# A pad of 192 bytes instead of 64 in front of the second phase's buffers: the spacing of matmuls whose weights load beside them

## The chip, the cores and the metric

The kernel runs on one core of a Trainium2 chip. What counts is the device time of one execution in microseconds, here the median of several runs. A second, profiled execution left the trace from which the rows below are taken. TensorE is called PE for its matmuls and PEld for its weight loads, VectorE DVE, ScalarE ACT, GpSimd POOL and SyncE SP.

## The reference, cut to what matters

One decoder layer on 512 positions of width 2048, all in float32. It mixes along time with a gated recurrence and with eight pairs of recurrent heads, then comes a feed-forward network of width 6144, then a gated embedding:

```python
h = h + jnp.concatenate([out_a, out_b], axis=-1) @ w_o[i]
u = rmsnorm(h, ln_ffn[i])
gate = causal_dwconv(u @ w_gate[i], conv_f_w[i], conv_f_b[i])
h = h + (jax.nn.gelu(gate) * (u @ w_up[i])) @ w_down[i]
u = rmsnorm(h, ln_ple[i])
e = jax.nn.sigmoid(u @ w_ple_gate[i]) * (p[i] @ w_ple_proj[i])
h = h + rmsnorm(e, ln_ple_post[i])
...
return rmsnorm(h, ln_final)
```

The change touches buffers of the last part alone: from the end of `w_o` to the final norm.

## The kernel before, in words

**Products.** Every large float32 product is made of three products of a shorter type: each operand is split into a high part, which ACT rounds (L138 for weights, L151 or L154 for activations), and a low part, which DVE makes as the difference (L139, L152, L155). PE then does high times high, high times low, low times high. Each of these three matmuls has its own weight load of 128 by 128 values, 512 bytes in each partition. PE loads the weights of the next matmul while the present one streams its moving operand.

**Stages.** Phase 1 is the mixing with its input products. Phase 2 starts with the second half of `w_o`, and has these stages:

- The gate and up products (`part`, L1281 to L1283). They are done by a scheme with seven products of quarters instead of eight. For each of 48 blocks of 128 columns there are seven units (`q5`, `p1`, `p4`, `p6`, `p7`, `p2`, `p3`), each with 8 steps of three matmuls. The stationary operand is a tile of weights (`whi`, `wlo`, or the pair x12 and x15). The moving operand is a form of the activations, 256 columns (1,024 bytes), and lies in the tiles s0 to s27. That is 48 x 7 x 24 = 8,064 matmuls.
- The down product (`product`, L1407 to L1409), 680 x 3 matmuls of 512 columns. Here the activations, in tiles s0 to s20, are stationary, and the weights `whi` and `wlo` move.
- The embedding's gate (`gate`, L1548 to L1550): activations stationary, most of them in s tiles and two of the sixteen in x13 and x14, weights moving. Three of the four column blocks are 512 wide, the last is done in two halves of 256.

**Where the tiles lie.** The memory of a partition is laid out by pools, one behind the other: `wp` with `whi` and `wlo`, `bp` with x0 to x15, then the pool of the phase, `k1` or `k2`; another pool stands at the far end. The tiles named here are 4,096 bytes each and follow without gaps. In the built program the first `whi` begins at byte 640, x0 at 25,216, and `k2` at 90,752, so that all three are at 128 modulo 256. The first thing in `k2` is a tile that nothing reads or writes, `skew` (L1227). It is 64 bytes long, and so all tiles behind it, s0 to s27 and the two buffers `e` among them, begin at 192 modulo 256. The offsets inside these tiles are multiples of 512 bytes, so that every operand of the three stages begins at the same place modulo 256 as its tile.

The order of the instructions is written out by hand in some stages and made by a scheduler with priorities in the others; the weights come by DMA from the SP and POOL queues, three units ahead.

Of the kernel before, what the change touches and what calls it, by code (L numbers as in the profile page):

```python
# [4 lines left out]
F32 = mybir.dt.float32  # L5
# [84 lines left out]
class Builder:  # L90
# [1125 lines left out]
    def phase2(self):  # L1216
        nc, A, k2 = self.nc, self.A, self.k2
# [6 lines left out]
        acc = self.t(self.cp, "row", (128, S + 2), bufs=1)[:, 0:S]  # L1224
        self.LOOK = 3
        hd = [self.dp.tile([128, 2, S], F32, name="hd%d" % i) for i in range(8)]
        self.skew = k2.tile([128, 16], F32, name="skew")  # L1227
        KIND = ("q5", "p1", "p4", "p6", "p7", "p2", "p3")
        X = {u: [T("s%d" % (4 * i + j), 1, (128, 2, 2, 256), F32R) for j in range(4)] for i, u in enumerate(KIND)}
        halves = lambda t: (t[:, 0:256], t[:, 256:512])  # L1230
# [513 lines left out]
```

## Time and profile before

| | us |
|---|---|
| three runs | 2582.25, 2549.99, 2585.5 |
| their median | 2582.25 |
| the profiled execution's own time | 2587.38 |
| its span, from the first to the last instruction | 2585.6 |
| PE busy | 2531.7 |
| DVE busy | 1902.7 |
| ACT busy | 1250.2 |

By stages, from the trace: phase 1 and the rest of `w_o` end at about 907 us, the gate and up products run from 907 to 1868 us, the down product from 1868 to 2372 us, the embedding and the final norm from 2372 us to the end.

A matmul's row in the trace shows a start and a duration. The durations overlap: a matmul of 256 columns is shown with 0.28 us, while the next starts 0.12 us later. So the rate of PE is read from the distance of the starts, or from a count of rows in a stretch in which PE is never idle, not from the duration of one row.

### The profile page before, as it was taken

What the parts mean: (1) busy time and instruction counts of PE and PEld (TensorE: products, weight loads), DVE (VectorE), ACT (ScalarE), POOL (GpSimd) and SP (SyncE); (2) the same over time, 40 slices, a digit from 0 to 9 for tenths busy, and PEclk for the clock granted to TensorE, in tenths of its full rate; (3) what the DMA queues carried; (4) which work ended last, traced back from release to release, by engine and by line L of the source; (5) the groups of instructions that cost most, each with busy time, mean ns of one, the idle gap of its engine ahead of it and who ended that gap; (6) DMA issues with size and microseconds to landing.
All of it is one profiled execution on the core that took longest, in us unless ns stands there. A gap on an engine that the chain in (4) does not pass through costs nothing.

```text
span 2585.6 us, 51614 instructions
## 1 busy us (share of the span) xinstructions
PE 2531.7 (98%) x21922; PEld 2221.2 (86%) x21922; DVE 1902.7 (74%) x2603; ACT 1250.2 (48%) x1735; POOL 228.3 (9%) x251
## 2 busy tenths in 40 slices
PE   9989999999999989999999999999999999999997
PEld 8867777777777889999999999999977878788887
DVE  5765775676675988888888887888876787896447
ACT  6563654547432644444444444444465453534345
POOL 0010100101031000000000000000000000000001
PEclk9989999999999999999999999999999999999999
DMA  7321222222342577767777667777678686843223
GB/s 255 94 70 59 87 78 67 79 87 71 98 137 87 172 209 185 190 168 197 188 187 193 187 170 195 193 187 196 188 214 252 180 228 179 237 117 115 93 91 111
DMA packets 131303, 393.76 MB, mean 152 GB/s; under 512 B 14464, under 2 KB 26624, under 8 KB 131072
## 3 DMA queue, kind: packets, MB, share of 16 engines
q1 hardware_dynamic: 96480, 299.22, 34.3%
q0 software_dynamic: 19872, 72.36, 16.8%
q10 hardware_dynamic: 14720, 18.88, 2.2%
q8 instruction: 171, 2.80, 0.4%
q14 instruction: 60, 0.49, 0.1%
HBM read 353.97 MB, written 36.44 MB: 151 GB/s over the span
## 4 chain that ended last, share of the span: by engine, by line
PE 68%; issue 18%; DVE 5%; ACT 5%; POOL 2%; DMA 1%; SPq 0%; POOLq 0%; ACTq 0%; DVEq 0%
PE mm L1282 8%; PE mm L1281 8%; PE mm L1283 8%; PE mm L168 5%; PE mm L170 5%; PE mm L172 5%; PE wk L1282 3%; PE wk L1281 3%; PE wk L1283 3%; PE mm L1548 2%; PE mm L1549 2%; PE mm L1550 2%; PE wk L833 1%; PE mm L1408 1%; PE mm L1409 1%
## 5 line engine op out<-in xcount | busy, mean ns | idle before, releaser
L138 ACT ACTIVATE whi<-x 128x1024 fp32r<-128x1024 f32 x329 | 349.0, 1061 | 481.6 <-PE mm L1282 222.8
L139 DVE TENSOR_TENSOR wlo<-x,whi 128x1024 fp32r<-128x1024 f32 x329 | 402.4, 1224 | 140.4 <-ACT whi L138 136.8
L138 ACT ACTIVATE whi<-wraw 128x1024 fp32r<-128x1024 f32 (+1 forms) x229 | 233.2, 1018 | 389.7 <-PE mm L170 186.4
L139 DVE TENSOR_TENSOR wlo<-wraw,whi 128x1024 fp32r<-128x1024 f32 (+1 forms) x229 | 278.3, 1215 | 174.6 <-ACT whi L138 173.2
L1281 PE MATMUL mm<-s,whi 128*128 128x256 f32 x1432 | 399.8, 279 | 2.4 <-ACT s L151 1.2
L1282 PE MATMUL mm<-s,whi 128*128 128x256 f32 x1432 | 401.0, 280 | 0.2 <-DVE s L152 0.2
L1283 PE MATMUL mm<-s,wlo 128*128 128x256 f32 x1432 | 399.7, 279 | 0.8 <-DVE wlo L139 0.8
L168 PE MATMUL mm<-x,whi 128*128 128x512 f32 x832 | 333.0, 400 | 1.4 <-DVE hT L458 0.9
L172 PE MATMUL mm<-x,wlo 128*128 128x512 f32 x832 | 332.7, 400 | 0.0
L170 PE MATMUL mm<-x,whi 128*128 128x512 f32 x832 | 331.0, 398 | 0.0
L1408 PE MATMUL mm<-wlo,s 128*128 128x512 f32 x680 | 270.5, 398 | 2.8 <-DVE wlo L139 2.8
L1281 PEld LDWEIGHTS mm<-s,whi 128*128 128x128 f32 x1432 | 269.2, 188 | 2.9 <-ACT s L151 1.4
L1407 PE MATMUL mm<-whi,s 128*128 128x512 f32 x680 | 269.6, 398 | 1.7 <-ACT whi L138 1.2
L1409 PE MATMUL mm<-whi,s 128*128 128x512 f32 x680 | 270.2, 397 | 0.1
L1282 PEld LDWEIGHTS mm<-s,whi 128*128 128x128 f32 x1432 | 268.8, 188 | 0.4 <-DVE s L152 0.4
L1283 PEld LDWEIGHTS mm<-s,wlo 128*128 128x128 f32 x1432 | 267.8, 187 | 1.0 <-DVE wlo L139 1.0
L168 PEld LDWEIGHTS mm<-x,whi 128*128 128x128 f32 x832 | 157.5, 189 | 37.3 <-issue 3.0
L170 PEld LDWEIGHTS mm<-x,whi 128*128 128x128 f32 x832 | 157.6, 189 | 33.9 <-issue 1.8
L172 PEld LDWEIGHTS mm<-x,wlo 128*128 128x128 f32 x832 | 157.2, 189 | 33.9 <-issue 1.9
L1281 PE MATMUL wk<-s,whi 128*128 128x256 f32 x584 | 163.9, 281 | 2.9 <-DVE e L1307 2.9
L1148 POOL DMA_DIRECT2D x<-wgu x94 | 82.7, 880 | 936.3 <-DVE wlo L139 638.6
L1282 PE MATMUL wk<-s,whi 128*128 128x256 f32 x584 | 164.2, 281 | 0.0
(588 smaller groups left out, 5415.1 us busy)
## 6 DMA issues: line engine op xcount, KB each, us to landing
x<-wgu SPq DMA_DIRECT2D x144, 512.0 KB, 4.2
x<-wgu POOLq DMA_DIRECT2D x94, 512.0 KB, 5.5
wraw<-wz SPq DMA_DIRECT2D x80, 512.0 KB, 3.5
wraw<-wgu SPq DMA_DIRECT2D x51, 512.0 KB, 4.4
x<-wd SPq DMA_DIRECT2D x49, 512.0 KB, 5.8
x<-wd POOLq DMA_DIRECT2D x44, 512.0 KB, 5.6
wraw<-wpg SPq DMA_DIRECT2D x31, 512.0 KB, 3.6
wraw<-wd SPq DMA_DIRECT2D x30, 512.0 KB, 4.5
```

Of the source, the lines that this page charges most:

```text
L138: nc.scalar.activation(hi, raw, AF.Copy)
L139: nc.vector.tensor_tensor(lo, raw, hi.bitcast(F32), ALU.subtract)
L168: nc.tensor.matmul(ps, hi[:, k, :], xh, start=first and i == 0, stop=False)
L170: nc.tensor.matmul(ps, hi[:, k, :], xl, start=False, stop=False)
L172: nc.tensor.matmul(ps, lo[:, k, :], xh, start=False, stop=last and i == n - 1)
L1148: nc.gpsimd.dma_start(g["s"], src(0, 0 if u == "p6" else 1), accum_op=ALU.add)
L1281: TE.matmul(ps, wh[:, k, :], xh, start=k == 0, stop=False)
L1282: TE.matmul(ps, wh[:, k, :], xl, start=False, stop=False)
L1283: TE.matmul(ps, wl[:, k, :], xh, start=False, stop=k == 7)
L1407: TE.matmul(ps, x[0][:, k, ts_], w[0][:, k, :], start=first and k == 0, stop=False)
L1408: TE.matmul(ps, x[0][:, k, ts_], w[1][:, k, :], start=False, stop=False)
L1409: TE.matmul(ps, x[1][:, k, ts_], w[0][:, k, :], start=False, stop=last and k == 1)
```

## The change

The tile `skew` is 48 values long instead of 16, which is 192 bytes instead of 64:

```diff
@@ -1224,7 +1224,7 @@
         acc = self.t(self.cp, "row", (128, S + 2), bufs=1)[:, 0:S]
         self.LOOK = 3
         hd = [self.dp.tile([128, 2, S], F32, name="hd%d" % i) for i in range(8)]
-        self.skew = k2.tile([128, 16], F32, name="skew")
+        self.skew = k2.tile([128, 48], F32, name="skew")
         KIND = ("q5", "p1", "p4", "p6", "p7", "p2", "p3")
         X = {u: [T("s%d" % (4 * i + j), 1, (128, 2, 2, 256), F32R) for j in range(4)] for i, u in enumerate(KIND)}
         halves = lambda t: (t[:, 0:256], t[:, 256:512])
```

Every tile of `k2` moves up by 128 bytes. In the built programs:

| tiles | before, byte | modulo 256 | after, byte | modulo 256 |
|---|---|---|---|---|
| whi, wlo, x0 to x15 | 640, 25,216 and on | 128 | the same | 128 |
| s0 to s27 | 90,816 and on | 192 | 90,944 and on | 64 |
| e (two buffers) | 205,504 and 209,600 | 192 | 205,632 and 209,728 | 64 |
| small tiles of the last stage | 213,696 and on | | 128 bytes higher | |

No instruction is added, removed or moved: the lists of all five engines are the same, row for row. Only the addresses of operands in `k2` differ.

## The prediction

> **What bounds the kernel now.** I read the page first, for the engine that is never idle, then a table of stages, then starts of matmuls.
>
> ```profile
> span 2585.6 us, 51614 instructions
> PE 2531.7 (98%) x21922; PEld 2221.2 (86%) x21922; DVE 1902.7 (74%) x2603; ACT 1250.2 (48%) x1735; POOL 228.3 (9%) x251
> core 0: us, PE busy (x) PEld busy (x) DVE busy (x) ACT busy (x) POOL busy (x), PEclk, DMA share, GB/s
> 907.00:950.00 43.00, 36.11 (x283) 34.87 (x281) 32.38 (x46) 17.79 (x27) 4.75 (x5) 0.96 0.72 215
> 950.00:1868.00 918.00, 918.00 (x7797) 918.00 (x7796) 757.37 (x840) 418.27 (x447) 79.93 (x92) 1.00 0.71 187
> 1868.00:2372.00 504.00, 499.41 (x2186) 400.03 (x2185) 387.97 (x433) 247.47 (x322) 38.76 (x44) 1.00 0.70 194
> 2372.00:2586.00 214.00, 197.19 (x1049) 167.34 (x1046) 112.84 (x199) 88.07 (x166) 7.19 (x8) 0.97 0.30 96
> ```
>
> The second window row is the one that matters: for 918 us, in the gate and up products, PE is never idle and its clock is full (1.00). 7,797 matmuls in 918 us are one every 117.7 ns. Nobody makes PE wait there, and DVE is at 757 of 918 us, or 83%. So this stage lasts exactly as long as PE needs from one start to the next. The down product is alike (499.4 of 504 us).
>
> The change moves no instruction, so its effect can only be in how long one takes. The question is whether the distance of two starts depends on where the operands lie. First, what overlaps with what; from the gate stage:
>
> ```profile
> 1199.83 0.28 PE L1281 MATMUL mm<-s,x 128*128 128x256 f32 x1
> 1199.84 0.19 PEld L1282 LDWEIGHTS mm<-s,x 128*128 128x128 f32 x1
> 1199.95 0.28 PE L1282 MATMUL mm<-s,x 128*128 128x256 f32 x1
> 1199.95 0.19 PEld L1283 LDWEIGHTS mm<-s,x 128*128 128x128 f32 x1
> ```
>
> The load for the next matmul starts with the present one, so each matmul reads two streams: its moving operand and the next one's weights. I call "relation" the place of the weights minus the place of the moving operand, modulo 256 bytes. In the gate stage the weights lie at 128 and the s tiles at 192: relation -64. In the down product and the embedding's gate the roles are exchanged, stationary s tiles at 192 and moving weights at 128: relation +64. The change turns -64 into +64 in the first and +64 into -64 in the other two.
>
> The trace of before has both relations at both widths. The last column block of the embedding's gate has 256 columns: relation +64 for s tiles, and 0 where both operands are s tiles:
>
> ```profile
> 2525.80 0.28 PE L1549 MATMUL mm<-wlo,s 128*128 128x256 f32 x1
> ...
> 2529.45 0.28 PE L1550 MATMUL mm<-whi,s 128*128 128x256 f32 x1
> ...
> 2530.35 0.38 PE L1548 MATMUL mm<-whi,s 128*128 128x256 f32 x1 [0.50 <-ACT e L1555]
> ...
> 2531.49 0.28 PE L1548 MATMUL mm<-whi,s 128*128 128x256 f32 x1
> ...
> 2541.92 0.28 PE L1548 MATMUL mm<-whi,s 128*128 128x256 f32 x1
> ...
> 2547.85 0.28 PE L1550 MATMUL mm<-s,s 128*128 128x256 f32 x1
> ...
> 2548.09 0.28 PE L1549 MATMUL mm<-s,s 128*128 128x256 f32 x1
> ...
> 2548.45 0.28 PE L1549 MATMUL mm<-s,s 128*128 128x256 f32 x1
> ...
> 2550.29 0.28 PE L1550 MATMUL mm<-whi,s 128*128 128x256 f32 x1
> ...
> 2551.99 0.28 PE L1550 MATMUL mm<-whi,s 128*128 128x256 f32 x1
> ```
>
> From 2525.80 to 2529.45 us there are 31 distances in 3.65 us: 117.7 ns. From 2531.49 to 2541.92 there are 92 in 10.43 us: 113.4 ns, with the same relation +64. At relation 0 (the rows `mm<-s,s`) there are 5 distances in 0.60 us: 120 ns. So the same form has three spacings, and +64 alone has been seen at two. Between the slower and the faster run at +64 stands one wait, for ACT, at 2530.35 us. The faster one holds until the relation changes. The last two rows are from the first of the last four passes, behind matmuls at relation 0: 15 distances in 1.70 us, again 113.3 ns.
>
> Now 512 columns. The first two rows are from the down product, relation +64; the other two from the gates of the recurrence in phase 1 (L1021 to L1025), whose moving operands lie at 192 and whose weights at 128, relation -64:
>
> ```profile
> 2107.86 0.39 PE L1409 MATMUL mm<-whi,s 128*128 128x512 f32 x1
> ...
> 2109.26 0.39 PE L1409 MATMUL mm<-whi,s 128*128 128x512 f32 x1
> ...
> 277.70 0.39 PE L1021 MATMUL wk<-lxh,whi 128*128 128x512 f32 x1
> ...
> 281.13 0.39 PE L1021 MATMUL wk<-lxh,whi 128*128 128x512 f32 x1
> ```
>
> 6 distances in 1.40 us are 233.3 ns at +64; 15 distances in 3.43 us are 228.7 ns at -64.
>
> **The change part by part.** The counts come from these groups; every one of their matmuls is there three times, on three lines:
>
> ```profile
> L1281 PE MATMUL mm<-s,whi 128*128 128x256 f32 x1432 | 399.8, 279 | 2.4 <-ACT s L151 1.2 <-ACT whi L138 1.2
> L1281 PE MATMUL wk<-s,whi 128*128 128x256 f32 x584 | 163.9, 281 | 2.9 <-DVE e L1307 2.9
> L1281 PE MATMUL mm<-s,x 128*128 128x256 f32 x488 | 136.2, 279 | 0.0
> L1281 PE MATMUL wk<-s,x 128*128 128x256 f32 x184 | 51.4, 279 | 0.0
> L1407 PE MATMUL mm<-whi,s 128*128 128x512 f32 x680 | 269.6, 398 | 1.7 <-ACT whi L138 1.2 <-ACT s L151 0.6
> L1548 PE MATMUL mm<-whi,s 128*128 128x512 f32 x168 | 66.7, 397 | 0.0
> L1548 PE MATMUL mm<-whi,s 128*128 128x256 f32 x96 | 26.8, 279 | 0.5 <-ACT e L1555 0.5
> L138 ACT ACTIVATE whi<-x 128x1024 fp32r<-128x1024 f32 x209 | 221.9, 1062 | 319.1 <-PE mm L1282 222.8 <-PE wk L1282 95.6 <-ACT x L1327 0.6
> ```
>
> Gate and up: 1432 + 584 + 488 + 184 = 2,688 on each of three lines, 8,064 in all, now 117.7 ns apart. At +64 the trace gives 113.4 or 117.7 ns, so the gain is 8,064 x 4.3 = 35 us or nothing. I take 113.4, because the longer stretch has it and the later pass settles at it, and because this stage runs 918 us without a wait that could throw it out. -35 us is the lower end; the third spacing, 120 ns, would add 8,064 x 2.3 = 19 us and is the upper end.
>
> Is there cover for a PE that is 4% faster? DVE would go from 83% to 86% of the stage and DMA from 0.71 to 0.74. The last row above, of ACT's weight splits between 950 and 1868 us, says that ACT was idle 319 us in front of them and waited for PE to give buffers back: the splits stand ready ahead of PE. So I cost this at nothing; if the cover went, the starts of the gate products would again carry waits as in the 43 us before 950.
>
> Down: 3 x 680 = 2,040 matmuls from 233.3 to 228.7 ns, -9.4 us. The row for -64 comes from stretches of a few us only; the ends are 0 and -9.4, and I take the measured one.
>
> Embedding's gate: 3 x 168 = 504 of 512 columns, -2.3 us by the same prices. 3 x 96 = 288 of 256 columns go to -64, whose spacing is the gate stage's 117.7; most of them have 113.4 now: +1.2 us. Those at relation 0 stay there, since both operands move together or neither does. DVE, ACT and DMA work on the moved tiles is unchanged in form and runs beside PE; I cost it at nothing, since in the gate stage none of it sets PE's time.
>
> Sum: -35 - 9.4 - 2.3 + 1.2 = -45.5 us. The profiled execution's own time is 2587.4 us, so it would be 2542. It lies 5 us above the median of the three runs, 2582.25, and so I forecast 2537 us for the median.
>
> [...]
>
> **The rivals.** The forecast, with the gate stage at 113.4 ns: chance 0.50.
>
> Stuck at 117.7: the two spacings at +64 show that something besides the relation decides, such as the moment at which a run of matmuls begins. The gate stage begins once, near 950 us, and keeps its spacing for 918 us, so it could be stuck in the slower one. Then only down and the embedding gain: 2582 - 10 = 2572 us. For it: the first of the three stretches at +64 above. Against it: the two later ones. Chance 0.24.
>
> No effect: place does not matter, or only modulo 128, where +64 and -64 are the same; the differences above would then come from what the matmuls work on. 2582 us. Against it: the three spacings appear within 25 us in one loop. [...] Chance 0.12.
>
> Slower: the pattern repeats at 512 bytes instead of 256. The gate stage's new relation is then 320, which no row shows at 256 columns, and it might behave as relation 0 does. It decides in the gate stage alone, and from the first matmul on: 8,064 x 2.3 = +19, less the 10 of the other stages (whose new relation, 192 modulo 512, is that of the phase 1 rows): 2591 us. Against it: the phase 1 and down rows fit modulo 256 as well. Chance 0.09.
>
> Both fast: the last 5% is that down goes further, to its width's share of the best spacing, 2 x 113.4 = 226.8 ns: another 2,040 x 1.9 = 4 us, 2533 us.
>
> **How the numbers follow.** The likeliest case is 2537. About 2% of 2582 is 52 us, which is about what a measurement here can tell from no change: faster means under 2530.6, slower over 2633.9. The three runs before lie 35 us apart, as much as the gate stage's whole gain, so runs of either spacing could mix; I allow 10 us to either side of the main case. From 2527 to 2583 the range holds the forecast, the stuck case and the case without effect; the slower rival and the far end of the main case are left out. Faster by over 2%: a third of the best case and a fifth of the main one, 0.12. Slower by over 2% would need the gate stage at over 124 ns, which no row shows: 0.03. The rest, 0.85, is within 2%.
>
> **What would show it.** In the trace of after: a stretch of the gate stage in which PE is never idle, with some 882 matmuls per 100 us (113.4 ns) instead of 850; a gate stage of about 926 us instead of 961; the down product at 228.7 ns; the last block's matmuls with s tiles at 117.7; phase 1 unchanged. The prediction is wrong if the gate stage stays at 117.7 or goes to 120, or if PE shows waits for DVE's `wlo` there.

## The result and the profile after

Twenty runs of each kernel, side by side: a median of 2581.64 us before and 2545.5 us after. The ratio is 0.986, with an interval from 0.983 to 0.989; by a bound of 2% that is no change. Eleven of the runs after lie between 2534 and 2547 us and nine between 2573 and 2582; before, 18 lie between 2577 and 2586 and two at 2546 and 2550. The ratio goes by the eleven alone, and leaves out the five longest of before; the means over all twenty are 2557.4 and 2578.8 us, a ratio of 0.992. That the same program has two times some 35 us apart is what the experiments take up.

The profiled execution took 2540.15 us, 47.2 less than the one of before (2587.38). The head of its page:

```profile
span 2538.4 us, 51614 instructions
PE 2480.6 (98%) x21922; PEld 2180.4 (86%) x21922; DVE 1899.3 (75%) x2603; ACT 1249.2 (49%) x1735; POOL 227.4 (9%) x251
```

PE is as full as before (98%), with as many matmuls, and 51 us less busy. The table of stages of after, with the same columns as before:

```profile
core 0: us, PE busy (x) PEld busy (x) DVE busy (x) ACT busy (x) POOL busy (x), PEclk, DMA share, GB/s
907.00:950.00 43.00, 35.57 (x286) 34.40 (x286) 31.87 (x39) 15.63 (x20) 4.86 (x5) 0.96 0.65 172
950.00:1830.00 880.00, 880.00 (x7754) 879.48 (x7753) 746.73 (x833) 414.11 (x441) 79.81 (x91) 1.00 0.74 195
1830.00:2330.00 500.00, 491.27 (x2187) 398.48 (x2185) 389.96 (x436) 249.41 (x326) 38.76 (x44) 1.00 0.71 196
```

The second row holds the gate and up products and the first 3 us of the down product. PE is never idle there, its clock is full (1.00), and 7,754 matmuls take 880 us. The starts of single matmuls show the spacing, and where it changes (timeline of after, PE; start and duration in us, line, tiles):

```profile
910.21 0.28 PE L1283 MATMUL mm<-s,wlo 128*128 128x256 f32 x1
...
913.04 0.28 PE L1283 MATMUL mm<-s,wlo 128*128 128x256 f32 x1
...
942.13 1.05 PE L210 MATMUL wk<-con,rsr 128*128 128x128 f32 x8
942.94 0.37 PE L1281 MATMUL wk<-s,x 128*128 128x256 f32 x1
943.15 0.28 PE L1282 MATMUL wk<-s,x 128*128 128x256 f32 x1
...
1826.92 0.28 PE L1283 MATMUL mm<-s,x 128*128 128x256 f32 x1
```

From 910.21 to 913.04 us there are 24 distances in 2.83 us: 117.9 ns, the spacing of before. Then come waits and other matmuls. The last of these are the eight of L210. Behind them a stretch begins that runs without a break from 943.15 to 1826.92 us: 7,798 distances in 883.77 us, 113.3 ns. In before, the last stretch of 7,798 begins behind the same L210 and runs at 117.8 ns. From its first matmul to its last, the gate and up stage lasts from 900.2 to 1826.9 us, 926.7 us; before it lasted from 907.1 to 1868.6, 961.4 us.

The down product and the last block of the embedding, from the same timeline:

```profile
2049.83 0.39 PE L1407 MATMUL mm<-whi,s 128*128 128x512 f32 x1
...
2052.35 0.39 PE L1409 MATMUL mm<-whi,s 128*128 128x512 f32 x1
...
2482.91 0.28 PE L1549 MATMUL mm<-wlo,s 128*128 128x256 f32 x1
...
2494.92 0.28 PE L1550 MATMUL mm<-whi,s 128*128 128x256 f32 x1
```

11 distances in 2.52 us are 229.1 ns (233.3 before). 102 distances in 12.01 us are 117.7 ns, at the relation that the gate stage had before.

### The profile page after: what moved, and what is told of

Read it like the earlier page. It is cut to its first block, busy times and chain, and to the rows that moved or that the text cites. A ratio compares the mean times of both kernels' runs of the same rounds, so it can differ in the third digit from the quotient of the medians.

```text
span 2538.4 us, 51614 instructions
## 1 busy us (share of the span) xinstructions
PE 2480.6 (98%) x21922; PEld 2180.4 (86%) x21922; DVE 1899.3 (75%) x2603; ACT 1249.2 (49%) x1735; POOL 227.4 (9%) x251
## 4 chain that ended last, share of the span: by engine, by line
PE 59%; DVE 6%; DMA 3%; ACT 2%; issue 1%; POOL 0%; ACTq 0%; POOLq 0%; DVEq 0%; SPq 0%
PE mm L1283 8%; PE mm L1281 8%; PE mm L1282 8%; PE mm L1409 5%; PE mm L1408 5%; PE mm L1407 5%; PE wk L1281 3%; PE wk L1283 3%; PE wk L1282 3%; PE mm L1548 2%; PE mm L1549 2%; PE mm L1550 2%; DVE wlo L139 2%; DMA wraw<-wd 2%; PE mm L168 1%
## 5 line engine op out<-in xcount | busy, mean ns | idle before, releaser
L138 ACT ACTIVATE whi<-wraw 128x1024 fp32r<-128x1024 f32 (+1 forms) x229 | 233.1, 1018 | 383.8 <-PE mm L170 168.6
L1281 PE MATMUL mm<-s,whi 128*128 128x256 f32 x1432 | 395.6, 276 | 2.7 <-ACT whi L138 2.0
L1282 PE MATMUL mm<-s,whi 128*128 128x256 f32 x1432 | 395.5, 276 | 0.2 <-DVE s L152 0.2
L1407 PE MATMUL mm<-whi,s 128*128 128x512 f32 x680 | 265.4, 392 | 4.1 <-ACT whi L138 2.9
L1409 PE MATMUL mm<-whi,s 128*128 128x512 f32 x680 | 268.6, 395 | 0.2
```

The lines of the kernel that those rows point to most:

```text
L138: nc.scalar.activation(hi, raw, AF.Copy)
L1281: TE.matmul(ps, wh[:, k, :], xh, start=k == 0, stop=False)
L1282: TE.matmul(ps, wh[:, k, :], xl, start=False, stop=False)
L1407: TE.matmul(ps, x[0][:, k, ts_], w[0][:, k, :], start=first and k == 0, stop=False)
L1409: TE.matmul(ps, x[1][:, k, ts_], w[0][:, k, :], start=False, stop=last and k == 1)
```

## The experiments

Distances below are means over a stretch, read from the starts of matmuls as above. All kernels here compute all that the kernel before computes; what is added writes to a column that nothing reads, or to a place that the real products write over afterwards.

### Starting the stretch 144 times

The long stretch starts once, so one execution shows one outcome. A matmul of one column, of the identity and a column of ones, in front of each of the 144 units `p1`, `p6` and `p7` breaks it up:

```diff
-                at = g[u] = (self.mm() if u == "p1" else self.aux())[:, 0:256]
+                bank = self.mm() if u == "p1" else self.aux()
+                at = g[u] = bank[:, 0:256]
+                TE.matmul(bank[:, 256:257], self.K("ident"), self.K("ones1"), start=True, stop=True)
```

Once with the pad of 192 bytes, relation +64:

> Pad of 192 bytes, and in front of every p1, p6 and p7 unit of the gate and up products a one-column float32 matmul into an unused column (its result is not used): 144 restarts of PE's stream in one run. Theory A (the relation allows two spacings and the start of a run of matmuls picks one): of the stretches between two restarts some stand at 113.3 ns and some at 117.7, more of the first. Theory B (the relation alone sets the spacing, and the 35 us between runs come from somewhere else): all stretches at 113.3. Theory C (the spacing wanders in time for a reason outside the kernel): stretches change in the middle, not at restarts. Time: some 144 x 0.1 to 0.3 us more than the kernel after.

and once with the pad of 64, relation -64:

> The same restarts with the pad of 64 bytes. Theory A: most stretches at 117.8 ns, a few at 113.3 (two of twenty runs of the kernel before were some 35 us faster). Theory B: all at 117.8.

Both were run once, with a profile. With the pad of 192 it took 2571.28 us, with the pad of 64 2593.43. Two windows rows, of PE alone; first the pad of 192:

```profile
1000.00:1800.00 800.00, 800.00 (x7040) 1.00 0.71 188
```

and the pad of 64, with the timeline around one of the added matmuls (L1304):

```profile
1000.00:1800.00 800.00, 800.00 (x6926) 1.00 0.70 184
```

and from its timeline:

```profile
1028.04 0.28 PE L1281 MATMUL mm<-s,whi 128*128 128x256 f32 x1
...
1035.82 0.28 PE L1281 MATMUL mm<-s,whi 128*128 128x256 f32 x1
...
1036.17 0.28 PE L1304 MATMUL mm<-con 128*128 128x1 f32 x2
...
1036.73 0.28 PE L1281 MATMUL mm<-s,x 128*128 128x256 f32 x1
...
1039.45 0.28 PE L1281 MATMUL mm<-s,whi 128*128 128x256 f32 x1
```

Ahead of the added matmul are 66 distances in 7.78 us, 117.9 ns; behind it 24 distances in 2.72 us, 113.3 ns. The next added matmul puts it back. With the pad of 64 the stretches alternate in this way nearly throughout, about 75 at 117.8 and 69 at 113.3. The expectation, most slower and a few faster, missed that. With the pad of 192, 142 of 144 run at 113.3, behind faster stretches and once behind a slower one; the other two lie in the first 40 us of the stage, where PE still has waits. By itself the run with the pad of 192 fits a relation that sets the spacing alone nearly as well. But relation -64 has both spacings, and they change where a stretch starts anew. The times are not those of a better kernel: the gate stage lasts 963.1 us with the pad of 192, against 926.7 with its spacing unbroken, so each break costs about 36.4 / 144 = 0.25 us.

### One start, chosen

Twelve extra matmuls stand in front of the last unit at which the stretch begins, (1, `p7`), behind L210. In lead A both operands are the weights' tile, in lead B both are the s tile. So with A, when the real products begin, the moving operand goes to another place; with B the stationary one does. The real products start from zero over the same place.

```diff
-        def part(ps, u):
+        def part(ps, u, lead=0):
             wh, wl = self.wnext()
+            for k in range(lead):
+                TE.matmul(ps, wh[:, k % 8, :], wh[:, 2 * (k % 4):2 * (k % 4) + 2, :].rearrange("p a b -> p (a b)"), start=True, stop=True)
...
-            part(at, u)
+            part(at, u, 12 if (n, u) == (1, "p7") else 0)
```

That is lead A. Lead B has in place of its two lines:

```diff
+            for k in range(lead):
+                xh = X[u][k // 2 % 4][:, k % 2, 0]
+                TE.matmul(ps, xh[:, 0:128], xh, start=True, stop=True)
```

Pad of 192, lead A and lead B:

> Pad of 192 bytes, and twelve matmuls of 256 columns at relation 0 (weights' tile x12 both as stationary and as moving operand, result overwritten) at the last restart before the long stretch of the gate and up products, some 1.4 us. The kernel before shows four passes that go from relation 0 to +64 with the stationary operand's place kept, and settle at 113.3 ns. Theory A: every run settles at 113.3 and takes about 2542 us, none 2576. Theories B and C: runs mix as they do without the twelve, 2540 and 2576, plus 1.4 us.

> The same with twelve matmuls at relation 0 made of an s tile with itself, so that it is the stationary operand's place that changes (64 to 128) when the stretch begins. The kernel before shows four short stretches like it, six matmuls each, at 117.7 ns. Theory A: every run is stuck at 117.7 in the gate stage and takes about 2577 us. Theories B and C: runs mix as without the twelve, plus 1.4 us.

Pad of 64, lead A and lead B:

> Pad of 64 bytes as in the kernel before, and the same twelve matmuls (weights' tile x12 with itself, relation 0) in front of the long stretch. Theory A (a start picks one of two spacings, at either relation): the stretch is the same in every run, at 113.3 or at 117.8 ns; if at 113.3 the time is about 2582 - 34 = 2548 us, some 9 us above the kernel after in its faster spacing, since the down product keeps 233.3 ns; if at 117.8 it is 2583. Theory D (relation -64 cannot hold the faster spacing for long, which the restarts showed only for up to 94 matmuls): 2583 us in every case.

> Pad of 64 bytes and twelve matmuls made of an s tile with itself. Theory A: again one spacing in every run, 2548 or 2583 us. One of this and the one before may well be at 113.3: with this pad the restarts gave both spacings, strictly in turn. Theory D: 2583 us.

| pad | relation in the gate stage | lead | median, us | lowest to highest | runs | ratio to before, interval |
|---|---|---|---|---|---|---|
| 192 | +64 | A | 2543.14 | 2538.51 to 2544.59 | 4 | 0.984 (0.982 to 0.986) |
| 192 | +64 | B | 2578.42 | 2573.67 to 2581.27 | 10 | 0.998 (0.997 to 0.999) |
| 64 | -64 | A | 2583.97 | 2576.62 to 2587.27 | 10 | 1.000 (0.999 to 1.001) |
| 64 | -64 | B | 2551.52 | 2549.73 to 2553.36 | 4 | 0.987 (0.985 to 0.988) |

In each of the four, all executions lie within 11 us. One windows row of PE from the same 860 us for each (span, PE busy, matmuls, clock, DMA). Before and after:

```profile
960.00:1820.00 860.00, 860.00 (x7304) 1.00 0.72 188
```

```profile
960.00:1820.00 860.00, 860.00 (x7590) 1.00 0.74 195
```

Pad of 192, lead A, then lead B with two rows of its down product:

```profile
960.00:1820.00 860.00, 860.00 (x7591) 1.00 0.74 194
```

```profile
960.00:1820.00 860.00, 860.00 (x7305) 1.00 0.72 188
```

and from its timeline:

```profile
2045.74 0.39 PE L1411 MATMUL mm<-wlo,s 128*128 128x512 f32 x1
...
2051.92 0.39 PE L1411 MATMUL mm<-wlo,s 128*128 128x512 f32 x1
```

Pad of 64, lead A, then lead B with two rows of its down product:

```profile
960.00:1820.00 860.00, 860.00 (x7304) 1.00 0.71 188
```

```profile
960.00:1820.00 860.00, 860.00 (x7591) 1.00 0.73 194
```

and from its timeline:

```profile
2045.84 0.39 PE L1410 MATMUL mm<-whi,s 128*128 128x512 f32 x1
...
2051.90 0.39 PE L1412 MATMUL mm<-whi,s 128*128 128x512 f32 x1
```

7,304 and 7,305 matmuls in 860 us are 117.7 ns, 7,590 and 7,591 are 113.3, and there is nothing between. Twelve matmuls, some 1.5 us of work, decide over the 880 to 920 us that follow, at either relation. With the same pad the choice alone is worth 2578.4 - 2543.1 = 35.3 us, or 2584.0 - 2551.5 = 32.5 us. The same lead has opposite effects at the two relations. In these four runs the stretch is the faster one where the operand that changes its place goes back by 64 bytes (A: from 128 to 64; B with the pad of 64: from 192 to 128), and the slower one where it goes forward by 64. That is a pattern of four cases and not a tested rule. How much each case proves differs. At the odds without a lead (11 of 20 in the shorter group with the pad of 192, 2 of 20 with the pad of 64), lead A's outcomes could be luck: four of four about one time in eleven, ten of ten about one in three. Lead B's could not: ten of ten in the longer group and four of four in the shorter, both against the odds, come by luck less than once in a thousand.

In the runs with leads the down product follows the relation alone. With lead B and the pad of 192, 27 distances in 6.18 us are 228.9 ns, although the gate stage is at 117.7; with the pad of 64, 26 distances in 6.06 us are 233.1 ns, although the gate stage is at 113.3. What is left of the change when the gate stage is held equal is 2551.5 - 2543.1 = 8.4 us (both at 113.3) and 2584.0 - 2578.4 = 5.6 us (both at 117.7). The two pads were not run side by side: the kernel before had a median of 2582.55 us beside the pad of 192 and 2584.04 beside the pad of 64, so some 1.5 us of either difference may not be the pad's.

### Other relations

The added one-column matmuls again, with a pad of 256 bytes (relation 0), of 320 (relation -64 modulo 256, but 192 modulo 512 instead of 448), and of 128 (s tiles at 0, weights at 128: relation 128). The edit for 256 bytes; the others have 80 and 32 values:

```diff
-        self.skew = k2.tile([128, 48], F32, name="skew")
+        self.skew = k2.tile([128, 64], F32, name="skew")
```

> Pad of 256 bytes and the restarts: relation 0. By the rows of the kernel before the gate stage stands at 120 ns in every stretch and the down product at 226.7 ns, so the gate stage is 8,064 x 2.2 = 18 us longer than in the slow spacing and the down product 13 us shorter than before. If two spacings belong to every relation, some stretches are below 120.

> Pad of 320 bytes and the restarts: relation -64 modulo 256 as with 64 bytes, but 192 instead of 448 modulo 512. If the pattern repeats at 256 bytes, the stretches take 113.3 and 117.8 ns in turn and the down product is at 233.3 ns, as with 64 bytes. If it repeats at 512, something else appears.

> The pad is 128 bytes, so that the s tiles and the weights' tiles both lie at 128 modulo 256 + their own 64: the relation is 128 in the gate product and in the down product alike, which no run has shown. The one-column matmuls in front of every unit are in, so the gate product starts 144 times. Theory (the relation sets which spacings a form can have, the start picks one of them): every gate stretch has one of the known spacings 113.3, 117.8 or 120.0 ns or a new one, and the down product, at one relation for all of its stretches, shows one value. If the price grows with the distance of the relation from 0, down lies above 233.3 ns; if the relations are a ring on which 0 and 128 are alike, it is 226.7 and the gate 120.0 in every stretch, as with the pad of 256. Rival (only the sign of the relation matters, its size does not): the gate alternates or settles as one of +64 and -64 does, and down is 229.0 or 233.3. Time by the spacings, from the 2617 us of the pad of 256 with its 120.0 and 226.7: all at 113.3 about 2617 - 8,064 x 6.7 ns = 2563, all at 120.0 about 2617.

They took 2617.37, 2596.31 and 2619.84 us. The pad of 256, with rows from one gate stretch and from the down product:

```profile
1000.00:1800.00 800.00, 800.00 (x6695) 1.00 0.67 179
```

and from its timeline:

```profile
1031.43 0.29 PE L1281 MATMUL wk<-s,x 128*128 128x256 f32 x1
...
1042.46 0.28 PE L1283 MATMUL mm<-s,wlo 128*128 128x256 f32 x1
...
2045.82 0.39 PE L1411 MATMUL mm<-whi,s 128*128 128x512 f32 x1
...
2049.22 0.39 PE L1411 MATMUL mm<-whi,s 128*128 128x512 f32 x1
```

92 distances in 11.03 us: 119.9 ns, and all 144 gate stretches have it. 15 distances in 3.40 us: 226.7 ns in the down product. Relation 0 is the slowest at 256 columns and the fastest at 512. The pad of 320, and the pad of 128 with rows from a gate stretch and from the down product:

```profile
1000.00:1800.00 800.00, 800.00 (x6928) 1.00 0.69 184
```

```profile
1000.00:1800.00 800.00, 800.00 (x6758) 1.00 0.68 180
```

and from its timeline:

```profile
1030.56 0.28 PE L1281 MATMUL wk<-s,x 128*128 128x256 f32 x1
...
1040.53 0.28 PE L1281 MATMUL mm<-s,whi 128*128 128x256 f32 x1
...
2046.01 0.39 PE L1409 MATMUL mm<-whi,s 128*128 128x512 f32 x1
...
2051.82 0.39 PE L1410 MATMUL mm<-wlo,s 128*128 128x512 f32 x1
```

With the pad of 320 the stretches alternate as with 64, 6,928 matmuls against 6,926, and down is at 233.3 ns. So at -64, the one relation tried, the pattern repeats at 256 bytes. At relation 128, 84 distances in 9.97 us are 118.7 ns, and no stretch settles at another spacing, though single distances go from 112 to 124 ns. In the down product 25 distances in 5.81 us are 232.4 ns. So the new relation has a value of its own at either width, and no better one. Only +64 and -64 have shown two.

### The places themselves, or only their differences

The pad of 64, and 64 bytes more in front of the weights' buffers, so that every tile of the products lies 64 bytes further (weights at 192, s tiles at 0 modulo 256), with the one-column matmuls:

```diff
             self.wp = top.enter_context(tc.tile_pool(name="wp", bufs=1))
+            self.front = self.wp.tile([128, 16], F32, name="front")
```

> A pad of 64 bytes stands in front of the weights' buffers, and the pad of before stands in front of the second phase's: every tile lies 64 bytes further than before, the weights at 192 and the s tiles at 0 modulo 256, and the relation in the gate product is -64, as before. The one-column matmuls are in. Theory (only the relation of the two streams counts): gate stretches alternate between 113.3 and 117.8 ns, down is 233.3 ns and the time is that of the kernel with the pad of 64 and the same one-column matmuls, 2593 us within 5. Rival (each operand's own place counts, modulo 256): another pattern, such as one spacing in every stretch, or another value of down.

It took 2611.2 us, as the rival had it for the gate stage:

```profile
1000.00:1800.00 800.00, 800.00 (x6804) 1.00 0.69 181
```

and from its timeline:

```profile
1028.48 0.28 PE L1305 MATMUL wk<-con 128*128 128x1 f32 x2
...
1028.83 0.28 PE L1283 MATMUL wk<-s,x 128*128 128x256 f32 x1
...
1039.89 0.28 PE L1284 MATMUL mm<-s,wlo 128*128 128x256 f32 x1
...
1040.01 0.28 PE L1305 MATMUL mm<-con 128*128 128x1 f32 x2
```

Between two added matmuls there are 94 distances in 11.06 us, 117.7 ns. 143 of 144 stretches have it, and none of them alternates; down is at 233.3. But the identity and the column of ones (`con`) had stayed at 96 modulo 256, so the relation between the added matmul and its neighbours had changed. A second run moves them too, by 192 bytes back, which is 64 forward modulo 256:

```diff
             self.con = cp.tile([128, CKEEP], F32, name="con")
+            self.back = cp.tile([128, 48], F32, name="back")
```

> As the run with every tile of the products 64 bytes further, and now the identity and the column of ones, which the one-column matmuls read, lie 64 bytes further modulo 256 as well (192 bytes back): every address that TensorE reads in the second phase is shifted alike, and every relation, those of the one-column matmuls to their neighbours too, is that of the kernel with the pad of 64 and the same one-column matmuls. There the gate stretches alternated; with only the products' tiles shifted they were all at 117.8 ns. Theory (only relations count, in the start of a stretch as well): the stretches alternate again between 113.3 and 117.8 ns, down is 233.3 ns, and the time is 2593 us within 5. Rival (the own place of the operands counts, modulo 256): they stay at 117.8 ns, 2611 us.

It took 2593.97 us:

```profile
1000.00:1800.00 800.00, 800.00 (x6926) 1.00 0.70 184
```

As many matmuls as with the pad of 64 and the same added matmuls, 6,926. The stretches alternate again, 74 slower and 70 faster, and down is at 233.4. With the pad of 64 every second stretch from the seventh on was the faster one, here every second from the eighth on, so the alternation is not tied to the place in the program. So in these runs what counts is how the places lie to each other, and that includes the few matmuls at the start. Moving `con` alone turned 143 stuck stretches into alternating ones, without a change in the gate products.

## Why the prediction was right, and where it was wrong

**What bounds the kernel** held: PE without a gap at a full clock (1.00 between 950 and 1868 us before and between 950 and 1830 us after), and a stage as long as its starts are apart. So did the view that these distances depend on where the operands lie: the one form with 256 columns was measured here at 120 ns at relation 0, at 118.7 at 128, and at 113.3 and 117.8 at +64 and -64.

**The gate and up products** were to give 35 us, and the profiled run gave 961.4 - 926.7 = 34.7. The size is right; the step that does not hold is "I take 113.4". The prediction saw that something besides the relation decides at +64, and took the faster spacing because the longer stretch had it and no wait could throw the stage out. But a stage without a wait keeps either spacing: with lead B the same addresses run at 117.7, and all ten executions take 2574 to 2581 us. Nor is 117.7 a property of -64, as the term for the embedding's last block supposed: with lead B and the pad of 64 the gate stage runs at 113.3. What the "stuck" rival said, that the beginning decides and holds for the whole stage, is what happens at either relation. The forecast had two spacings seen at +64 and only one at -64, and read the latter as the only one. The kernel of before had shown a second: its three runs lay 35 us apart, as the prediction noted. Its two shortest times among the twenty, 2546.1 and 2550.0 us, lie up to 4 us below and at the 2549.7 to 2553.4 us that the pad of 64 takes when it is led into 113.3. That the groups of runs of before and after are these two spacings is inferred from such times, since a trace exists of one execution of each only. If so, the change moves the odds of a good start, from 2 in 20 to 11 in 20, and adds a smaller gain that comes with the places alone. What makes the start differ between executions of one program was not found. That the profiled run and the median show the faster spacing was therefore in part luck: one execution more in the longer group would have put the median midway between the two groups, two more at some 2573 us, near the "stuck" case.

**The down product** was to give 9.4 us, and its spacing went to 229.0 ns as the rows of phase 1 had said. The stage, from first to last start, went from 497.4 to 493.5 us: 3.9. Waits and long distances behind them took most of the rest. The waits of PE in this stage, before and after (us in total, times, longest):

```profile
PE mm L1408 <- DVE wlo L139: 2.8, 5, 0.8
PE mm L1407 <- ACT whi L138: 1.2, 2, 0.8
PE mm L1407 <- ACT s L151: 0.6, 1, 0.6
```

```profile
PE mm L1408 <- DVE wlo L139: 3.4, 6, 0.8
PE mm L1407 <- ACT whi L138: 2.9, 4, 1.6
PE mm L1407 <- ACT s L151: 1.2, 1, 1.2
```

4.6 us became 7.5. Behind a wait the distances without one can be long too: in before 334 ns behind the wait of 0.8 us that ends at 2218.5 us, and 426 or 427 ns seven times in a row from 2098.74 us on, just behind two waits of 0.8 us, with a granted clock of 0.61 from 2097.5 to 2101.8 us. With the waits, the distances over 260 ns exceed 230 ns by 10.3 us in all before and by 14.8 after. The prediction asked for the cover of the gate stage, where it held, and not for that of the down product, where PE waits for the splits. The kernels of the experiments show that these waits vary: this excess is between 4.4 and 14.8 us in the thirteen profiles. Where it was alike, in the two runs with the one-column matmuls (6.8 us with the pad of 64, 6.4 with 192), the stage went from 493.9 to 485.0 us, 8.9 us shorter and close to the forecast. Between the runs with leads, where it was 5 to 7 us larger with the pad of 192, the stage got only 3.1 and 1.9 us shorter. So the gain per matmul was right, and the cover for it was missing; why the waits differ so between kernels was not found.

**The embedding's gate** was to give 2.3 - 1.2 = 1.1 us, and went from 196.8 to 195.5 us.

**The sum**, 45.5 us, lies close to the 47.2 of the profiled runs, but not by its own terms: 34.7 + 3.9 + 1.3 + 0.3 behind it are 40.2. The other 6.9 us come from ahead of the gate stage, which began at 900.2 us instead of 907.1. That is not the change: over the 13 profiles here it begins anywhere from 900.2 to 909.1 us, with the same phase 1. The median after, 2545.5, lies 8.5 us above the forecast and inside the range.

**The rivals.** "No effect" fell with the rows of after. The slower one, with a pattern that repeats at 512 bytes, fell with the rows of after, where no stretch of the gate stage settles at 120 ns, and with the pad of 320. "Both fast" had its 226.7 ns, but at relation 0, where the gate stage has 120.

**The best version** is the pad of 192 with lead A: 2538.5 to 2544.6 us in all four runs, 1.6% (1.4 to 1.8) below the kernel before. Against the plain change it is not faster at its best, but it was so each of the four times, which the plain change would do about one time in eleven.

## What to carry to other kernels

Where PE runs without a gap at a full clock, divide the time by the number of matmuls and compare like forms across the trace. Here the spacing went from 113.3 to 120.0 ns at 256 columns and from 226.7 to 233.3 ns at 512, with where the weights and the moving operand lie to each other modulo 256 bytes (that it repeats there was tried at -64 alone), and at 256 columns also with the start of the stretch; a pad tests it. If the times of one program fall into two groups, look for a long stretch with no break whose spacing differs between executions; here twelve matmuls at its start went with one group alone, in all four or all ten runs of each version. Before a gain in spacing is counted, ask in each stage whether the operands come that much earlier, and do not take a spacing that was seen once for the only one its layout has.

## What the runs showed of the hardware

- The matmul with 256 columns and a weight load beside it had these steady spacings: 120.0 ns at relation 0, 118.7 at 128, and 113.3 or 117.8 at +64 and at -64. With 512 columns there was one value for each relation: 226.7 ns at 0, 229.0 at -64, 233.3 at +64, and 232.4 at 128.
- At +64 and -64 the spacing went with the twelve matmuls at the start (7,591 or 7,304 to 7,305 matmuls in the same 860 us), and in before and after it was kept for 7,798 distances. Beside it DVE, ACT and DMA went on: DVE was busy 746.7 us and ACT 414.1 us of 880 us after, with DMA at a share of 0.74.
- The one-column matmul between stretches led to the faster spacing at +64 in 142 of 144 stretches, and at -64, after the first few, to the other one than before; with the identity moved by 64 bytes against the other tiles, at -64, it led to the slower one in 143 of 144 stretches.
- At -64, 256 bytes more of pad changed neither spacing (6,928 matmuls in 800 us instead of 6,926), and a common shift of all operands by 64 bytes left both as they were (6,926).
